# An encoder block on Trainium2: first and second gate products ahead of the third, merge loads behind branch A's last values, another tile order, operands realigned

## The chip, the cores and the metric

One core of one Trainium2 chip runs the whole program. The metric is the device time of one execution in microseconds (us). TensorE is called PE here, VectorE DVE, ScalarE ACT, GpSimd POOL, and SyncE, which issues most of the transfers (DMAs), SP.

## The reference

An encoder block on 1024 tokens of width 1024, with 16 meta tokens in front, in float32. Two attention branches read the same normalised input: A is a differential attention over all 1040 keys (4 heads, each with two softmaxes whose second is subtracted with a weight), B a grouped attention over a window with sinks. Each branch has a gate per element, a projection of the same input. After the merge come an output projection and a SwiGLU feed-forward network (FFN).

```python
h = jnp.concatenate([meta, x], axis=1)
# mixer_block(rms_norm(h)):
proj = h @ w_in                       # qa, ka, va, qb, kb, vb, ga, gb
y_a = differential_attention(qa, ka, va, ...)   # softmax(s1) - lam * softmax(s2), ALiBi bias
y_b = windowed_gqa(qb, kb, vb, sink)
merged = jax.nn.sigmoid(ga) * (y_a @ w_ba) + jax.nn.sigmoid(gb) * (y_b @ w_bb)
h = h + merged @ w_o
# swiglu(rms_norm(h)):
h = h + (jax.nn.silu(h @ w_gate) * (h @ w_up)) @ w_down
return rms_norm(h, norm_final)[:, N_META:]
```

## The kernel before, in words

**Arithmetic.** Every matrix operand is split into a high and a low float32 part (`split`, L116: ACT writes the high part, another engine the difference), and a product is three matmuls: high × high, high × low, low × high. The large products (gates, output projection, FFN) follow a Strassen–Winograd scheme: seven products of halves, numbered p = 1, 2, 6, 5, 7, 3, 4, in place of eight, with sums of halves before and after.

**Stages.** In the time of the trace: projections and branch B to about 294 us; branch A from there to 626 us, with the gate products filled in; the merge (`branch_w` L709, `branch_mm` L716, `gated` L1192) to 735 us; output projection and FFN norm to 816 us; FFN gate and up products (L1568) to 1243 us; down products (L1672) to the end.

**Branch A** runs over 32 tiles (head h, block t of 128 queries). `scores_a` (L922) makes for each of two softmaxes (m = 1, then 0) three chunks of scores, 352, 352 and 336 keys: the first two into the double bank `two` (one buffer), the third into a bank with the tag `sc` (three buffers). DVE adds the bias and takes the minimum (L942, L946), ACT takes the exponential (L950), and DVE combines the two (L956). `transpose_a` (L961) then turns the 1040 keys of that tile in blocks of four, four and one, again through `sc`, which ACT (L971) and DVE (L972) empty. `values_a` (L975) multiplies with the values for two tiles at a time, and `normed_a` (L985) norms four tiles. `load_a` (L900) loads queries and keys of a head (`aq`, `ak`) from DRAM.

**Gate products.** There are 8 pairs k of output columns with seven products each (`order_g`, L728–730). One product is four steps of three matmuls (`gate_steps`, L817, matmul at L850); its weights are loaded by `load_g` (L745), put together by `weights_g` (L759: p = 6 needs two sums on POOL, L779 and L780, p = 1 and 2 none) and split. p = 1 is kept in `u` tiles, p = 2 is stored, p = 6 is added to the kept p = 1 and stored to DRAM (`u_d`, L864), and is loaded again for the later products. The moving operand is the transposed input `hT_hi`, `hT_lo`, of whose four quarters (half of the contraction × half of the tokens) three are overwritten, one of them twice, by prepared sums `t_d`, here called T0, T1, T2 and T3: `turn_into` (L808). RIGHT_G (L802) says which quarter a product reads: p = 1 and 5 the quarter that T0 replaces, p = 2 and 4 that of T3, p = 3 the quarter that stays, and p = 6 and 7 the quarter of T2 and then T1. T0, T1 and T3 can come only when the first products of all pairs no longer need what lies there.

**Order.** The order of PE's instructions in branch A is written by hand: the string SLOTS (L41) gives the order in one tile, with s for a chunk of this tile's scores, t for a third of the tile before's transposition, n for a step of the tail (values, norm), g for one gate step. Ahead of a head stand G_FIRST = 24 (first head) or G_HEAD = 6 gate steps (L54), and HOLD = 22 steps are kept for the end. The order on the other engines, and that of the transfers on SP's queue, is set by a scheduler with a timeline of its own.

**Merge.** Its first loads are two blocks of `w_bb` (L711 into `m0`) and eight of `yb` (L1138 into `m1`); each `yb` block is split by ACT (L117) and DVE (L118) before the first matmul at L719. The loads of gates `gt` are issued at L1195, their sigmoid runs on ACT at L1196.

Of the kernel before, what the change touches and what calls it, by code (L numbers as in the profile page):

```python
# [37 lines left out]
N_WAIT = 3  # L38
PP2 = 2
COMBINE_POOL = (0, 1, 2, 3)  # L40
SLOTS = "ssgsgssgsngtntgnt"  # L41
SLOTS_LAST = "ssgsgssgsngtntgnt"
S_BUFS = (2, 2)
AT_BUFS = 2
G_BUFS = 3
HOLD = 22
GT_BUFS = 4
WB_BUFS = 6
# [25 lines left out]
def encoder_block(ctx: ExitStack, tc: tile.TileContext, x, meta, norm_mix, w_in, lq1, lk1, lq2, lk2,  # L74
# [7 lines left out]
    def f32(ap):  # L82
        return ap.bitcast(F32)
# [27 lines left out]
    ones = const.tile([P, 1], F32, name="ones")  # L111
    nc.gpsimd.memset(ones, 1.0)
    neg_half = const.tile([P, 4], F32, name="neg_half")
    nc.gpsimd.memset(neg_half, -0.5)

    def split(hi, lo, src, lo_eng):  # L116
# [591 lines left out]

    def branch_w(p, o, src, nme, raw=None, low=None):  # L709
        w = (raw_tile(f"wbr{nme}_{o}")[:, 0:512] if raw is None else raw).rearrange("p (c n) -> p c n", n=P)  # L710
        nc.sync.dma_start(w, src[:, o * P:(o + 1) * P].rearrange("(c p) n -> p c n", p=P))  # L711
        wh = p.tile([P, 2, 4, P], F32R, tag="wh", name=f"wbh{nme}_{o}", bufs=WB_BUFS)
        split(wh[:, 0], wh[:, 1], w, low or nc.gpsimd)
        return wh
# [11 lines left out]


    G_COLS = [C_GB + 2 * k * P for k in range(4)] + [C_GA + 2 * k * P for k in range(4)]  # L728
    first_g = [(k, p) for i in (0, 2) for p in (1, 2) for k in (i, i + 1)] + [(k, 6) for k in range(4)]
    first_g += [(k, p) for k in range(4, 8) for p in (1, 6, 2)]  # L730
    order_g = first_g + [(k, p) for k in range(8) for p in (5, 7, 3, 4)]
    n_first = len(first_g)

# [1 line left out]
    for n, (k, p) in enumerate(order_g):  # L735
        if n >= n_first:
            uses_g.append([("s", k, 1), ("s", k, 0)] if p == 5 else [])
        elif k < 4:
            uses_g.append({1: [("f", k, 0)], 2: [], 6: [("m", k, 0), ("m", k, 1)]}[p])
        else:  # L740
            uses_g.append({1: [("f", k, 0)], 2: [], 6: [("f", k, 1)]}[p])
    loads_g = [u for us in uses_g for u in us]
    raw_g, ops_g, n_loaded, n_freed, n_made = {}, {}, [0], [0], [0]

# [14 lines left out]
    def weights_g(n):  # L759
        k, p = order_g[n]  # L760
        load_g()
        tt = nc.gpsimd.tensor_tensor
        nm = f"{k}_{p}"
        kind = "s" if n >= n_first else "f" if k >= 4 or p != 6 else "m"
        wa, wb = raw_g[kind, k, 0], raw_g.get((kind, k, 1))
        a11, a12 = wa[:, 0:4], wa[:, 4:8]
        if wb is not None:
            a21, a22 = wb[:, 0:4], wb[:, 4:8]
        done = []
        if p == 1:  # L770
            src = a11
        elif p == 2:
            src, done = a12, ["f"]
            if k < 4:
                n_freed[0] += 1
            else:
                n_freed[0] += 2
        elif p == 6:
            tt(a21, a21, a22, ALU.add)  # L779
            tt(a21, a21, a11, ALU.subtract)  # L780
            src = a21
            if k < 4:
                n_freed[0] += 2
        elif p == 5:
            src = sums_g[k] = gstage.tile([P, 4, P], F32, tag="s", name=f"s1g_{k}", bufs=1)
            tt(src, a21, a22, ALU.add)
        elif p == 7:
            tt(a21, a11, a21, ALU.subtract)
            src = a21
        elif p == 3:  # L790
            tt(a12, a12, a11, ALU.add)
            tt(a12, a12, sums_g.pop(k), ALU.subtract)
            src = a12
        else:
            src = a22
# [7 lines left out]
            n_made[0] += 1  # L803

    RIGHT_G = {1: (0, 0), 6: (0, 1), 2: (1, 0), 5: (0, 0), 7: (0, 1), 3: (1, 1), 4: (1, 0)}
    INTO_T = {2: (0, 1), 0: (0, 0), 1: (0, 1), 3: (1, 0)}

    def turn_into(i):  # L808

        d, t = INTO_T[i]  # L810
        for hl, h in enumerate((hT_hi, hT_lo)):
            with ExitStack() as after:
                if i == 2:
                    after.enter_context(tc.issue_after(keys_a[0].ins))
                nc.sync.dma_start(f32(h)[:, 4 * d:4 * d + 4, HALF[t]], t_d[i][:, hl])

    def gate_steps():  # L817
        banks, kept = {}, {}
# [10 lines left out]
        add = nc.vector.tensor_tensor  # L829
        for n, (k, p) in enumerate(order_g):  # L830
            ensure_g(n + 1)
            if n == n_first - 4:
                kept[0] = kept_g("u_0")
                nc.sync.dma_start(kept[0], u_d[0])
            if n >= n_first - 1 and p in (2, 4) and (n < n_first or k < 7):
# [12 lines left out]
            for c in range(4):  # L848
# [3 lines left out]
                                     stop=(p in (2, 6, 3, 4) and c == 3 and i == 2), skip_group_check=True)  # L852
                if c == 3:
                    if p == 1:
                        kept[k] = kept_g(f"p1_{k}")
                        nc.scalar.copy(kept[k], ps)
                    elif p == 2:
                        st = stage_g(f"g11_{k}")
                        nc.scalar.copy(st, ps)
                        store(st, 2 * k, 0)  # L860
                    elif p == 6:
                        u = kept.pop(k)
                        add(u, ps, u, ALU.add)
                        nc.sync.dma_start(u_d[k], u)  # L864
                    elif p == 5:
                        kept["q"] = kept_g(f"q_{k}")
                        nc.scalar.copy(kept["q"], ps)
                    elif p == 7:
                        st = stage_g(f"g22_{k}")
                        add(st, ps, kept.pop("q"), ALU.add)  # L870
                        store(st, 2 * k + 1, 1)
                    else:
                        st = stage_g(f"g{p}_{k}")
                        if p == 3:
                            nc.scalar.copy(st, ps)
                        else:
                            add(st, ps, kept[k], ALU.add)
                        store(st, 2 * k + (p == 4), int(p == 3))
                    if n + 1 == n_first - 2:
                        turn_into(0)  # L880
                    elif n + 1 == n_first - 1:
                        turn_into(1)
                    elif n + 1 == n_first:
                        turn_into(3)
                    if p == 4:
                        del kept[k]
                    if p == 7 and k < 7:
                        kept[k + 1] = kept_g(f"u_{k + 1}")
                        nc.sync.dma_start(kept[k + 1], u_d[k + 1])
# [94 lines left out]

    def normed_a(h, c, py):  # L985
        nm = f"{h}_{c}"
        ysq = apool.tile([P, 512], F32, tag="ysq", name=f"ysq_{nm}", bufs=1)
        nc.scalar.activation(ysq, py, AF.Square)
        yg = apool.tile([P, 512], F32, tag="yg", name=f"yg_{nm}", bufs=2)
        nc.scalar.activation(yg, py, AF.Copy, scale=gsub)  # L990
        yield
        pst = bank(psum2, "sc", f"apst_{nm}", SC)
# [24 lines left out]
            next(gates, None)  # L1017


    acc = [None]  # L1020

    def turn(done):
        h, t, s, at_, v = done
# [2 lines left out]
    def later(done):  # L1026
        h, t, s, at_, v = done
        if t % 4 == 1:
            acc[0] = bank(psum2, "acc", f"apy_{h}_{t}", 1)
        yield from values_a(h, t, v, at_, acc[0])  # L1030
        if t % 4 == 3:
            yield from normed_a(h, t // 4, acc[0])

# [40 lines left out]
    while tail:  # L1074
        step_tail()
        fill(1)
    order_pe.__exit__(None, None, None)
    close_apool()
    fill(1000)
    bops, close_bops = pool("bops")  # L1080

    def half_op(p, name):
# [2 lines left out]
    def block_pair(i, name, dtype):  # L1085
        return bops.tile([P, 2, 4, 512], dtype, tag=f"x{i}", name=name, bufs=1)

    ypool, close_ypool = pool("ypool")
    close_psum2()
    close_stage()  # L1090
# [31 lines left out]
    m0, m1, ya0 = block_pair(0, "m0", F32), block_pair(1, "m1", F32), block_pair(2, "ya0", F32R)  # L1122
    a11, asum, a12, w11 = m0[:, 0], m0[:, 1], m1[:, 0], m1[:, 1]

    def merged(o, half):
        return ((a11, a21), (a12, a22))[o // 4][half][:, o % 4]

# [5 lines left out]

    yb_t = []
    for j in range(4):
        raws_b = a12[:, j], w11[:, j]
        for h in range(2):
            nc.sync.dma_start(raws_b[h], yb_d[j][:, h * 512:h * 512 + 512])  # L1138
# [666 lines left out]
```

## Time and profile before

| | us |
| --- | --- |
| three runs | 1461.11, 1463.01, 1465.54 |
| median | 1463.01 |
| profiled execution | 1460.98 |
| its span in the profile | 1458.9 |
| PE busy | 1419.6 (97%) |
| DVE, ACT, POOL busy | 913.6, 704.8, 603.2 |

Mean granted clock of PE: 0.987. The profile shows one execution. A line of a group names the line of the kernel, the engine, the operation, output <- inputs, the shape and the count, then busy time, mean ns of one, and the engine's idle time just before with what ended it. In a timeline the first two columns are start and length; a bracket gives the idle time before and its releaser. Matmuls overlap: the length of one (389 ns) is more than the distance to the next (about 230 ns). A name of a queue (SPq) marks the issue of a transfer, not its time in flight.

### The profile page before, as it was taken

To read this page: it belongs to the slowest core of one execution; us is meant where nothing else is said; L and a number is where in the kernel's file an instruction comes from. 1 tells how busy PE (TensorE), PEld (TensorE's weight loads), DVE (VectorE), ACT (ScalarE), POOL (GpSimd) and SP (SyncE) were. 2 spreads that over 40 slices of the span, in tenths; PEclk is the share of its full clock that TensorE was granted. 3 is DMA by queue.
4 is the path that set the end of the run, shared out by engine and by line. 5 is a ranking of instruction groups with operands and counts; after the bars stand their busy time and mean duration, and the time that the engine had idled before them with its cause. 6 is when DMAs were issued, how large, how long until landed. Compare 5 with 4: busy or idle time off the path is not lost.

```text
span 1458.9 us, 20686 instructions
## 1 busy us (share of the span) xinstructions
PE 1419.6 (97%) x7183; PEld 1209.3 (83%) x7183; DVE 913.6 (63%) x1584; ACT 704.8 (48%) x1340; POOL 603.2 (41%) x591
## 2 busy tenths in 40 slices
PE   9999999988999999979999999999999999999998
PEld 8998999976888888868888888888888888888886
DVE  6555666526676767735978866754455443787666
ACT  6355556434565555545345654333333333444444
POOL 4157866228364645230513135544544542000442
PEclk9999999998999999989999999999999999999999
DMA  8445564396558344186351633433333322964444
GB/s 235 97 123 154 165 194 136 101 292 202 168 191 261 128 148 150 44 295 205 131 178 58 195 107 110 144 123 97 100 100 104 99 94 102 327 221 135 132 124 144
DMA packets 190696, 222.98 MB, mean 153 GB/s; under 512 B 17064, under 2 KB 125040, under 8 KB 190592
## 3 DMA queue, kind: packets, MB, share of 16 engines
q1 hardware_dynamic: 188672, 218.84, 47.6%
q10 hardware_dynamic: 1920, 2.83, 0.7%
q8 instruction: 56, 0.92, 0.3%
q14 instruction: 48, 0.39, 0.1%
HBM read 150.64 MB, written 64.42 MB: 147 GB/s over the span
## 4 chain that ended last, share of the span: by engine, by line
PE 87%; DVE 5%; DMA 4%; ACT 2%; issue 1%; SPq 1%; POOL 0%; ACTq 0%; DVEq 0%; POOLq 0%
PE pg L1568 29%; PE pd L1672 14%; PE pg L850 6%; PE ppa L719 5%; PE po L1471 4%; PE aps L939 3%; PE pp_va L228 3%; PE pp_qb L228 3%; PE pp_qa L228 3%; PE apy L981 3%; PE pp_ka L228 3%; DMA ak<-ka_d 2%; PE bps L395 2%; PE po L1479 2%; PE bpy L435 1%; PE bpt L430 1%
## 5 line engine op out<-in xcount | busy, mean ns | idle before, releaser
L1568 PE MATMUL pg<-t,wop 128*128 128x512 f32 x1056 | 242.8, 389 | 0.0
L1568 PEld LDWEIGHTS pg<-t,wop 128*128 128x128 f32 x1056 | 198.2, 188 | 41.8
L118 POOL TENSOR_TENSOR wop<-wf,wop 128x512 fp32r<-128x512 f32 x114 | 152.7, 1341 | 168.1 <-ACT wop L117 156.2
L1672 PE MATMUL pd<-ob,oa 128*128 128x512 f32 x924 | 209.6, 389 | 0.0
L1672 PEld LDWEIGHTS pd<-ob,oa 128*128 128x128 f32 x924 | 173.4, 188 | 36.1 <-DVE ob L118 0.2
L1568 PE MATMUL pg<-b,wop 128*128 128x512 f32 x792 | 188.5, 395 | 0.0
L850 PE MATMUL pg<-hT_hi,wopg 128*128 128x512 f32 x448 | 174.7, 410 | 8.5 <-ACT wopg L117 7.8
L1568 PEld LDWEIGHTS pg<-b,wop 128*128 128x128 f32 x792 | 148.0, 187 | 36.1
L117 ACT ACTIVATE wop<-wf 128x512 fp32r<-128x512 f32 x128 | 80.8, 633 | 76.7 <-PE pg L1568 54.2
L950 ACT ACTIVATE as<-as,amn 128x1040 f32<-128x1040 f32 x64 | 74.4, 1163 | 64.9 <-DVE amn L946 64.7
L850 PEld LDWEIGHTS pg<-hT_hi,wopg 128*128 128x128 f32 x448 | 87.0, 194 | 22.4 <-ACT wopg L117 8.5
L118 POOL TENSOR_TENSOR oa<-ra,oa 128x512 fp32r<-128x512 f32 x27 | 34.9, 1294 | 168.9 <-ACT oa L117 167.4
L939 PE MATMUL aps<-ak,aq 128*128 128x352 f32 (+1 forms) x384 | 88.5, 338 | 13.1 <-DVE at L972 6.5
L117 ACT ACTIVATE oa<-ra 128x512 fp32r<-128x512 f32 x77 | 48.7, 632 | 107.9 <-PE pd L1672 45.6
L939 PEld LDWEIGHTS aps<-ak,aq 128*128 128x128 f32 x384 | 66.2, 192 | 30.7 <-DVE at L972 7.9
L942 DVE CUSTOM_DVE_ANT_0 as<-aps,dist,far_a 128x704 f32<-128x704 f32 x64 | 60.4, 944 | 48.2 <-PE aps L939 48.2
L850 PE MATMUL pg<-hT_lo,wopg 128*128 128x512 f32 x224 | 89.9, 402 | 0.0
L1345 DVE TENSOR_TENSOR s<-wf,wf 128x512 f32<-128x512 f32 x22 | 15.7, 714 | 114.8 <-DMA wf<-in_w_ff_up_dram 72.2
L397 DVE CUSTOM_DVE_ANT_0 bs<-bps,tbx,nsink 128x432 f32<-128x432 f32 (+1 forms) x64 | 38.5, 627 | 56.4 <-PE bps L395 35.0
L407 POOL TENSOR_SCALAR bs<-bs,bdn 128x432 f32<-128x432 f32 (+1 forms) x64 | 37.0, 597 | 76.7 <-DVE bdn L405 48.9
L1595 ACT COPY p<-pg 128x512 f32<-128x512 f32 x44 | 25.8, 585 | 66.5 <-PE pg L1568 62.3
L981 PE MATMUL apy<-at,av 128*128 128x256 f32 x400 | 57.4, 287 | 0.0
(320 smaller groups left out, 3148.5 us busy)
## 6 DMA issues: line engine op xcount, KB each, us to landing
ra<-aop SPq DMA_DIRECT2D x77, 256.0 KB, 2.7
wf<-in_w_ff_gate_dram SPq DMA_DIRECT2D x25, 512.0 KB, 3.9
wf<-in_w_ff_up_dram SPq DMA_DIRECT2D x25, 512.0 KB, 3.8
aop<-as SPq DMA_DIRECT2D x44, 256.0 KB, 2.2
w_c<-in_w_in_dram SPq DMA_DIRECT2D x17, 512.0 KB, 4.9
aop<-c SPq DMA_DIRECT2D x33, 256.0 KB, 2.0
t_d<-tst SPq DMA_DIRECT2D x16, 512.0 KB, 3.9
g_d<-g SPq DMA_DIRECT2D x32, 256.0 KB, 3.6
```

Source lines behind the costliest of these rows:

```text
L117: high = nc.scalar.activation(hi, src, AF.Copy)
L118: lo_eng.tensor_tensor(lo, src, f32(hi), ALU.subtract)
L228: product = nc.tensor.matmul(ps[:, :n], a[:, c, :], b[:, c, at:at + n], start=(u == 0), stop=(u == 3 * DC - 1))
L719: nc.tensor.matmul(ps, w[:, a, j, :], src(j, b, tk), start=(j == 0 and n == 0), stop=(j == 3 and n == 2))
L850: nc.tensor.matmul(ps, op[:, x, c, :], h[:, 4 * d + c, HALF[t]], start=(p in (1, 6, 7) and c == 0 and i == 0), stop=(p in (2, 6, 3, 4) and ...
L939: nc.tensor.matmul(ps[:, :n], qs[m][:, t * P:(t + 1) * P], ks[m][:, vv, k0:k0 + n], start=(vv == 0), stop=(vv == 1))
L942: nc.vector.tensor_tensor_reduce(s[m][:, 0:2 * n].rearrange("p (a k) -> p a k", a=2), two[:, :, :n], dist[:, u0:u0 + 2 * n].rearrange("p ( ...
L950: nc.scalar.activation(s[m][:, 0:L], s[m][:, 0:L], AF.Exp, bias=mn[:, m, 1:2], scale=-1.0, accum_out=dn[:, 1:2] if m else first_sum)
L981: nc.tensor.matmul(py[:, cols], v[:kp, a, k, :], at_[:kp, k, b, :], start=(k == 0 and j == 0), stop=(k == 8))
L1471: nc.tensor.matmul(sets_o[p][u], oa[:, a, u * P:(u + 1) * P], ob[:, b, :], start=(p in (1, 5) and j == 0 and k == 0), stop=(p in (2, 3) an ...
L1568: nc.tensor.matmul(ps, op[:, x, c, :], b[:, y, c, :], start=(p in (1, 5) and c == 0 and n == 0), stop=(p in (4, 2, 3) and c == 3 and n == ...
L1672: nc.tensor.matmul(ps[u], oa[:, a, u * P:(u + 1) * P], ob[:, b, :], start=(p in (1, 2, 5) and j == 0 and k == 0), stop=(p in (2, 3, 4) and ...
```

## The change

It has four parts.

1. A tile of 64 bytes for each partition, `room`, is allocated among the constants and never used. Tiles allocated after it on the left side of SBUF start 64 bytes further on.
2. The gate products p = 1 and p = 2 of all eight pairs come first, then p = 6 of all eight. Results of p = 1 go to DRAM and are loaded again one product ahead of its use. Every pair takes its p = 6 weights with two loads of its own (before: pairs 4 to 7 reused a load). T0 is loaded after product (7, 1), T3 in eight transfers during (7, 2), T1 after (7, 6); before, T0, T1 and T3 came with the last three of the first 24 products.
3. In a tile's order, the first n and the first t stand ahead of the second half of the scores.
4. The merge's first loads are issued as soon as the last values of branch A have been given out; branch A's pool is closed there, and two of its tiles (`ysq`, `yg`) move to another pool.

```diff
-SLOTS = "ssgsgssgsngtntgnt"
+SLOTS = "ssgsgntssgsgntgnt"
...
+ROOM = 16
...
+    const.tile([P, ROOM], F32, name="room")
...
-        nc.sync.dma_start(w, src[:, o * P:(o + 1) * P].rearrange("(c p) n -> p c n", p=P))
+        if raw is None:
+            nc.sync.dma_start(w, src[:, o * P:(o + 1) * P].rearrange("(c p) n -> p c n", p=P))
...
-    first_g = [(k, p) for i in (0, 2) for p in (1, 2) for k in (i, i + 1)] + [(k, 6) for k in range(4)]
-    first_g += [(k, p) for k in range(4, 8) for p in (1, 6, 2)]
+    first_g = [(k, p) for i in (0, 2, 4, 6) for p in (1, 2) for k in (i, i + 1)] + [(k, 6) for k in range(8)]
...
-        elif k < 4:
+        else:
             uses_g.append({1: [("f", k, 0)], 2: [], 6: [("m", k, 0), ("m", k, 1)]}[p])
-        else:
-            uses_g.append({1: [("f", k, 0)], 2: [], 6: [("f", k, 1)]}[p])
...
+    LAST_T = {(7, 1): 0, (7, 2): 3, (7, 6): 1}
...
-        for hl, h in enumerate((hT_hi, hT_lo)):
-            with ExitStack() as after:
-                if i == 2:
-                    after.enter_context(tc.issue_after(keys_a[0].ins))
-                nc.sync.dma_start(f32(h)[:, 4 * d:4 * d + 4, HALF[t]], t_d[i][:, hl])
+        for c in (range(4) if i == 3 else (slice(0, 4),)):
+            for hl, h in enumerate((hT_hi, hT_lo)):
+                with ExitStack() as after:
+                    if i == 2:
+                        after.enter_context(tc.issue_after(keys_a[0].ins))
+                    to = f32(h)[:, 4 * d:4 * d + 4, HALF[t]]
+                    nc.sync.dma_start(to[:, c], t_d[i][:, hl, c])
...
-            if n == n_first - 4:
-                kept[0] = kept_g("u_0")
-                nc.sync.dma_start(kept[0], u_d[0])
+            for k_next in [0] * (n in (n_first - 9, n_first - 2)) + [k + 1] * (p == 6 and k < 7):
+                kept[k_next] = kept_g(f"u_{k_next}")
+                nc.sync.dma_start(kept[k_next], u_d[k_next])
...
                     if p == 1:
-                        kept[k] = kept_g(f"p1_{k}")
-                        nc.scalar.copy(kept[k], ps)
+                        p1 = kept_g(f"p1_{k}")
+                        nc.scalar.copy(p1, ps)
+                        nc.sync.dma_start(u_d[k], p1)
...
-                    if n + 1 == n_first - 2:
-                        turn_into(0)
-                    elif n + 1 == n_first - 1:
-                        turn_into(1)
-                    elif n + 1 == n_first:
-                        turn_into(3)
+                    if (k, p) in LAST_T:
+                        turn_into(LAST_T[k, p])
...
-        ysq = apool.tile([P, 512], F32, tag="ysq", name=f"ysq_{nm}", bufs=1)
+        ysq = gstage.tile([P, 512], F32, tag="ysq", name=f"ysq_{nm}", bufs=1)
...
+        if (h, t) == (AH - 1, NT - 1):
+            valued.append(t)
...
     n_gates[0] += HOLD
+    while not valued:
+        step_tail()
+        fill(1)
+    close_apool()
+    bops, close_bops = pool("bops")
...
+    for o, raw in enumerate((a11[:, 2], asum[:, 0])):
+        nc.sync.dma_start(raw.rearrange("p (c n) -> p c n", n=P), w_bb[:, o * P:(o + 1) * P].rearrange("(c p) n -> p c n", p=P))
+    for j in range(4):
+        for h in range(2):
+            nc.sync.dma_start((a12, w11)[h][:, j], yb_d[j][:, h * 512:h * 512 + 512])
     while tail:
         step_tail()
         fill(1)
     order_pe.__exit__(None, None, None)
-    close_apool()
     fill(1000)
```

More of the change, by code (lines that the diff above doesn't have):

```diff
@@ L40 @@
 COMBINE_POOL = (0, 1, 2, 3)
-SLOTS = "ssgsgssgsngtntgnt"
-SLOTS_LAST = "ssgsgssgsngtntgnt"
+SLOTS = "ssgsgntssgsgntgnt"
+SLOTS_LAST = "ssgsgntssgsgntgnt"
 S_BUFS = (2, 2)
@@ L763, in weights_g @@
         nm = f"{k}_{p}"
-        kind = "s" if n >= n_first else "f" if k >= 4 or p != 6 else "m"
+        kind = "s" if n >= n_first else "m" if p == 6 else "f"
         wa, wb = raw_g[kind, k, 0], raw_g.get((kind, k, 1))
@@ L768, in weights_g @@
             a21, a22 = wb[:, 0:4], wb[:, 4:8]
-        done = []
         if p == 1:
@@ L772, in weights_g @@
         elif p == 2:
[L773 to L777, printed above, removed]
+            src = a12
+            n_freed[0] += 1
         elif p == 6:
@@ L781, in weights_g @@
             src = a21
-            if k < 4:
-                n_freed[0] += 2
+            n_freed[0] += 2
         elif p == 5:
@@ L831, in gate_steps @@
             ensure_g(n + 1)
-            if n == n_first - 4:
-                kept[0] = kept_g("u_0")
-                nc.sync.dma_start(kept[0], u_d[0])
-            if n >= n_first - 1 and p in (2, 4) and (n < n_first or k < 7):
+            for k_next in [0] * (n in (n_first - 9, n_first - 2)) + [k + 1] * (p == 6 and k < 7):
+                kept[k_next] = kept_g(f"u_{k_next}")
+                nc.sync.dma_start(kept[k_next], u_d[k_next])
+            if n == n_first - 1 or (p == 4 and k < 7):
                 nxt = 0 if n < n_first else k + 1
@@ L986, in normed_a @@
         nm = f"{h}_{c}"
-        ysq = apool.tile([P, 512], F32, tag="ysq", name=f"ysq_{nm}", bufs=1)
+        ysq = gstage.tile([P, 512], F32, tag="ysq", name=f"ysq_{nm}", bufs=1)
         nc.scalar.activation(ysq, py, AF.Square)
-        yg = apool.tile([P, 512], F32, tag="yg", name=f"yg_{nm}", bufs=2)
+        yg = gstage.tile([P, 512], F32, tag="yg", name=f"yg_{nm}", bufs=2)
         nc.scalar.activation(yg, py, AF.Copy, scale=gsub)
@@ L1017, in fill @@
             next(gates, None)
-    acc = [None]
+    acc, valued = [None], []
     def turn(done):
@@ L1073, in encoder_block @@
     n_gates[0] += HOLD
-    while tail:
+    while not valued:
         step_tail()
         fill(1)
-    order_pe.__exit__(None, None, None)
     close_apool()
-    fill(1000)
     bops, close_bops = pool("bops")
@@ L1086, in block_pair @@
         return bops.tile([P, 2, 4, 512], dtype, tag=f"x{i}", name=name, bufs=1)
+    m0, m1, ya0 = block_pair(0, "m0", F32), block_pair(1, "m1", F32), block_pair(2, "ya0", F32R)
+    a11, asum, a12, w11 = m0[:, 0], m0[:, 1], m1[:, 0], m1[:, 1]
+    for o, raw in enumerate((a11[:, 2], asum[:, 0])):
[3 more added lines that the diff above has]
+            nc.sync.dma_start((a12, w11)[h][:, j], yb_d[j][:, h * 512:h * 512 + 512])
+    while tail:
+        step_tail()
+        fill(1)
+    order_pe.__exit__(None, None, None)
+    fill(1000)
     ypool, close_ypool = pool("ypool")
@@ L1121, in encoder_block @@
     a21, a22 = (keep.tile([P, 4, 512], F32, name=f"m_{n}") for n in ("21", "22"))
-    m0, m1, ya0 = block_pair(0, "m0", F32), block_pair(1, "m1", F32), block_pair(2, "ya0", F32R)
-    a11, asum, a12, w11 = m0[:, 0], m0[:, 1], m1[:, 0], m1[:, 1]
     def merged(o, half):
@@ L1135, in encoder_block @@
     for j in range(4):
-        raws_b = a12[:, j], w11[:, j]
-        for h in range(2):
-            nc.sync.dma_start(raws_b[h], yb_d[j][:, h * 512:h * 512 + 512])
         yb_t.append(ybpool.tile([P, 2, S], F32R, name=f"yb{j}"))
```

## The prediction, given before the changed kernel was run

> **What bounds the kernel now.** I read the page first: busy time, clock, and the chain that ended last.
>
> ```profile
> PE 1419.6 (97%) x7183; PEld 1209.3 (83%) x7183; DVE 913.6 (63%) x1584; ACT 704.8 (48%) x1340; POOL 603.2 (41%) x591
> ...
> PEclk9999999998999999989999999999999999999999
> ...
> PE 87%; DVE 5%; DMA 4%; ACT 2%; issue 1%; SPq 1%; POOL 0%; ACTq 0%; DVEq 0%; POOLq 0%
> ```
>
> TensorE (PE) is busy for 97% of the span and holds 87% of the chain. The other engines matter only where PE waits for them. So there are three places to gain: idle time of PE, stretches at a lower clock (the two slices marked 8), and the pitch of the matmuls themselves. The waits of PE between 300 and 660 us, next, list all idle time that the change can reach (total, times, longest, in us).
>
> ```profile
> PE ppa L719 <- ACT yb L117: 7.9, 1, 7.9
> PE pg L850 <- ACT wopg L117: 7.8, 2, 6.0
> PE aps L939 <- DVE at L972: 6.5, 7, 2.1
> PE aps L939 <- DVE amn L942: 3.3, 7, 1.0
> PE aps L939 <- DMA ak<-ka_d: 3.2, 3, 1.7
> PE ppa L719 <- DVE yb L118: 0.6, 1, 0.6
> PE pg L850 <- POOL wopg L118: 0.5, 1, 0.5
> ```
>
> That is 29.8 us: 8.5 where the merge starts, 6.0 and 2.3 where a gate product waits for its weights, 9.8 at score matmuls that wait for a PSUM bank or buffer, 3.2 for keys still in flight. A longer stall costs clock as well. These are stretches from the windows view: length, busy time of PE, PEld, DVE, ACT, POOL, clock, DMA share, GB/s.
>
> ```profile
> 332.00:338.00 6.00, 5.88 (x19) 4.58 (x20) 1.66 (x3) 2.00 (x4) 4.71 (x4) 0.50 0.77 209
> ...
> 365.50:367.40 1.90, 1.90 (x7) 1.61 (x7) 1.01 (x4) 0.61 (x1) 0.69 (x1) 0.51 0.00 0
> ...
> 508.90:512.30 3.40, 3.40 (x13) 3.11 (x13) 1.85 (x7) 1.35 (x3) 0.07 (x1) 0.50 0.00 0
> 644.40:648.80 4.40, 3.80 (x8) 2.68 (x9) 4.40 (x7) 4.40 (x9) 0.76 (x1) 0.50 1.10 351
> ```
>
> PE works there at 0.50 of its clock, so half of each stretch is lost.
>
> **The change, part by part.** The sum is made against the profiled execution (1460.98 us, span 1458.9).
>
> *A, operands realigned.* The 64-byte tile `room` shifts what lies above it on the left side of SBUF. By the allocated addresses, the three moving operands `b` of FFN products (L1568) start at 64 modulo 128 before and at 0 after; their stationary operand `wop` starts at 0 in both. The same stationary tile with the moving operand `t`, at 0 already, is the comparison; `yb`, too, is out of step with its weights and `ya` is not.
>
> ```profile
> L1568 PE MATMUL pg<-t,wop 128*128 128x512 f32 x1056 | 242.8, 389 | 0.0
> L1568 PE MATMUL pg<-b,wop 128*128 128x512 f32 x792 | 188.5, 395 | 0.0
> ...
> L719 PE MATMUL ppa<-yb,wbhb 128*128 128x512 f32 x192 | 45.8, 401 | 8.5 <-ACT yb L117 7.9 <-DVE yb L118 0.6
> L719 PE MATMUL ppa<-ya,wbha 128*128 128x512 f32 x192 | 44.0, 390 | 0.2 <-DVE wbha L118 0.2
> ```
>
> `b` matmuls cost 6 ns more than `t` matmuls: 792 × 6 ns = **−4.75 us**. By busy time, 188.5/792 − 242.8/1056 = 8.1 ns, so −6.4 at most; nothing if alignment isn't the cause.
>
> *B, start of branch A.* The gate product that stood ready least was p=6 of pair 0: its two raw loads and two GpSimd sums came before its split.
>
> ```profile
> 323.97 0.80 PE L939 MATMUL aps<-ak,aq 128*128 128x352 f32 x4
> ...
> 331.78 0.80 PE L850 MATMUL pg<-hT_hi,wopg 128*128 128x512 f32 x1 [6.01 <-ACT wopg L117]
> ...
> 324.12 1.30 DVE L956 SCALAR_TENSOR_TENSOR as<-as,adn,as 128x1040 f32<-128x1040 f32 x1
> ```
>
> After the change p=1 or p=2 of a later pair stands there, which splits a loaded half without a sum. The 6.0 us go, and with them the half clock of 332 to 338 (6 us at 0.50: 3 us lost). Late next is the first transposition, which now stands ahead of tile 1's second scores (at 323.97) and needs tile 0's combination (324.12 + 1.30 = 325.42): 1.5 us, with a hand-over some 1.7, and about 1.4 for a short clock stretch. Net **−5.9** (−9 to 0).
>
> *C, the tiles.* With `t` earlier, score banks are evicted earlier (L972), so most of the 9.8 us at L939 goes, and two clock stretches of 3.4 us like that at 509.
>
> ```profile
> 365.30 0.69 PE L939 MATMUL aps<-ak,aq 128*128 128x336 f32 x2 [2.12 <-DVE at L972]
> ...
> 386.46 0.47 PE L939 MATMUL aps<-ak,aq 128*128 128x336 f32 x2
> 386.77 0.39 PE L850 MATMUL pg<-hT_hi,wopg 128*128 128x512 f32 x1
> ...
> 387.47 0.60 PE L968 MATMUL apt<-ident,as 128*128 128x128 f32 x4
> ...
> 389.47 1.24 PE L981 MATMUL apy<-at,av 128*128 128x256 f32 x9
> ...
> 389.46 1.30 DVE L956 SCALAR_TENSOR_TENSOR as<-as,adn,as 128x1040 f32<-128x1040 f32 x1
> ```
>
> The new exposure is the softmax. The last scores of tile 7 start at 386.46 and its combination ends at 389.46 + 1.30 = 390.76: 4.3 us. In the new order PE has between these four gate steps (386.77 to 387.47: 0.70 each, 2.8), the next tile's three score parts (1.1 by the rows of tile 7 in D), the rest of a transposition (0.5) and one or two parts of values (1.1 each): 5.5 to 6.6 us. That covers it; I keep 5.7 us for new waits, 0.7 in each of the eight tiles in which the row sums' own transposition (L1005) still holds a score bank. 9.8 + 2 × 1.7 − 5.7 = 7.5: **−7.5** (−12 to +15, the latter in the rivals).
>
> The rows disagree here with the Trainium skill, "TensorE: Matmul & The Clock Gate", Part 1 on the HAM clock gate: it has the clock fall after an idle window of about 3.4 us. Here a wait of 2.12 us was followed by 0.51. By the page the two stretches would have another cause, and this term would be some 3 us smaller.
>
> *D, the boundary of heads 0 and 1.* This speaks against the change. Keys and queries of head 1 are loaded during tile 7. So far little is queued before them on SP; the last keys are 1.04 us late.
>
> ```profile
> 383.99 0.34 SPq L906 DMA_DIRECT2D aq<-qa_d  x1
> ...
> 387.82 1.11 SPq L909 DMA_DIRECT2D ak<-ka_d  x2
> ```
>
> ```profile
> 382.01 0.89 PE L939 MATMUL aps<-ak,aq 128*128 128x352 f32 x4
> ...
> 397.10 0.32 PE L939 MATMUL aps<-ak,aq 128*128 128x352 f32 x1
> 398.46 0.75 PE L939 MATMUL aps<-ak,aq 128*128 128x352 f32 x3 [1.04 <-DMA ak<-ka_d]
> ```
>
> The quarters T0 and T3 of hT (2.1 MB each) used to be reloaded well after that, in a stretch of their own:
>
> ```profile
> 425.56 0.38 SPq L815 DMA_DIRECT2D hT_lo<-t_d  x1
> 426.04 0.46 SPq L815 DMA_DIRECT2D hT_hi<-t_d  x1
> ```
>
> And the DMA view of 424 to 446:
>
> ```profile
> DMA packets 4050, 6.49 MB, mean 295 GB/s; under 512 B 124, under 2 KB 1148, under 8 KB 4047
> ...
> hT_hi<-t_d SPq DMA_DIRECT2D x3, 1024.0 KB, 8.2
> ```
>
> Now all 16 first and second products come first, so T0 is free after (7,1) and T3 after (7,2), in tiles 6 and 7. In SP's new order T0, five transfers of 256 KB, two weight loads of 512 KB and the eight chunks of T3 stand ahead of or between head 1's loads: with these (3.1 MB), 10.2 MB from T0 to the last keys. The window above moved 6.49 MB in 22 us, 2 of them idle: 325 GB/s. 10.2 MB take 31 us; T0 is issued some 5 us before tile 7's start, so the last keys land 26 us after it and are needed at 397.1 − 382.0 = 15.1: 11 us of stall. At 400 GB/s it would be 5.5. I take 10, nearer the measured rate, less today's 1.0, plus 2.5 for the clock (half of a 5 us stretch): **+11.5** (0 to +16).
>
> *E, T1* is loaded after (7,6) now, one product ahead of (0,7), which uses it. Cover: four of a tile's five gate steps, and 32 tiles take 302 us (324 to 626): 4/5 × 9.4 = 7.5. Load: 8.2 us to landing (the last row above) and 1.6 for a 512 KB weight load in front: 9.8. **+3** with its clock (0 to +5).
>
> *F, merge's loads* move from 627.43 to the end of the last values, some 6 us earlier. But ACT's order keeps four sigmoids and a weight split ahead of the first `yb`:
>
> ```profile
> 627.43 0.99 SPq L711 DMA_DIRECT2D m<-in_w_branch_b_dram  x2
> ...
> 640.38 2.72 ACT L1196 ACTIVATE gt<-gt 128x512 f32<-128x512 f32 x4 [4.72 <-DMA gt<-g_d]
> 643.17 0.63 ACT L117 ACTIVATE wbhb<-wbrb 128x512 fp32r<-128x512 f32 x1
> 643.71 4.25 ACT L117 ACTIVATE yb<-m 128x512 fp32r<-128x512 f32 x8
> ```
>
> Their `gt` loads are not moved ahead by as much; I expect the first `yb` at about 641: **−3** (−8 to 0).
>
> *At nothing:* eight more stores and eight loads of 256 KB and four of 512 KB, 6 MB in all, elsewhere hidden under the gate steps (if that cover goes, as in D); matmul, GpSimd and ACT counts are equal.
>
> Sum: −4.75 − 5.9 − 7.5 + 11.5 + 3 − 3 = −6.65. The profiled execution would take 1454.3 us; it stands 2.0 below the median of 1463.01, so I predict **1456**.
>
> **The rivals.**
>
> *R1, head 1's loads arrive in time,* because the transfers move faster than in the window above or T0 goes out sooner. For it: some half-microsecond slices of that window reach 400 GB/s and over. Against it: 10.2 MB in 20 us would need 510. D falls to +1 at most, and E may shrink: 1456 − 12 = 1444.
>
> *R2, slower: the softmax becomes the bound of each tile.* Where the first `t` comes before the combination of the tile before is done, PE waits in every tile; it decides from the point where the latency is above the cover of 5.5 to 6.6 us. With half a us in each of 30 tiles, +15: 1471. For it: DVE and ACT also get the evictions of `t` in the same stretch, in front of the exponential. Against it: 4.3 us in the rows above.
>
> *R3, the realignment does nothing:* `b` matmuls stay at 395 because of something else in those products. Then 1456 + 4.75 = 1461. Against it: `t` and `b` share weights, shape and line. The Trainium skill speaks for this rival: "TensorE: Matmul & The Clock Gate", Step-by-step, gives PE two independent read ports, one for the moving operand and one for weights, so that where the two lie relative to each other should not matter. The rows at 389 and 395 agree with this only if something other than the address separates them.
>
> **How the numbers follow.** Chances: the forecast 0.50 (its own range 1450 to 1462), R1 0.25, R2 0.13, R3 0.12. A measurement of this kernel tells a difference of 0.3% (4.4 us) from none. Faster by more than that, under 1458.6, are R1, and about three quarters of the forecast: 0.62. Slower, over 1467.4, is most of R2: 0.12. The rest, 0.26, is R3 and the forecast's upper end. The range takes in R1 and its better side of F, and the nearer part of R2: 1440 to 1470.
>
> **What the profile after would show.** A: `pg<-b` at 389. B: no wait of 6 us near 325, instead `apt` waiting for DVE at L956. C: L939 without DVE waits; if `apt` waits in most tiles, R2. D: a wait of `aps` for DMA of 8 to 12 us at tile 8, with a clock of 0.5 behind it; under 3 us means R1. E: a wait for `hT` near 510. F: the merge's wait for `yb` at 4 to 5 us. The forecast fails most easily in D: it hangs on one rate.

## The result, and the profile after

| | before | after |
| --- | --- | --- |
| runs, us | 1461.11 to 1467.81 (5) | 1450.25 to 1455.74 (5) |
| median, us | 1464.21 | 1452.44 |
| profiled execution, us (span) | 1460.98 (1458.9) | 1455.20 (1453.4) |

The ratio is 0.9922, with a 95% interval from 0.9898 to 0.9947: faster by 7.8 to 14.9 us, where 6.65 in a profiled execution and 1456 as the median were forecast. The executions of one kernel differ by 5 to 7 us here, and by 14 in the longest series (27 runs of before, 1458.1 to 1472.0). The profiled execution of before was faster than all five of its runs in the table, and that of after slower than three of the other four, so the 5.8 us between these two probably understate the gain. Sums of terms go by this profiled pair, and kernels are compared by their ratios to before, which was run again on the chip of each.

The page of after: busy time, clock by slice, and the chain.

```profile
PE 1413.3 (97%) x7183; PEld 1210.1 (83%) x7183; DVE 914.0 (63%) x1584; ACT 702.2 (48%) x1340; POOL 604.3 (42%) x591
...
PEclk9999999999999999999999999999999999999999
...
PE 83%; DMA 6%; DVE 4%; SPq 2%; issue 2%; ACT 1%; POOL 1%; ACTq 0%; DVEq 0%; POOLq 0%
```

PE is busy 6.3 us less for the same 7183 matmuls. DMA and SP's queue have 8% of the chain in place of 5%: transfers now end waits that others ended before. PE's waits between 300 and 660 us show which.

```profile
PE aps L934 <- DMA ak<-ka_d: 6.3, 2, 4.8
PE ppa L722 <- ACT yb L119: 6.2, 1, 6.2
PE apt L963 <- DVE at L967: 4.7, 5, 2.0
PE apt L963 <- DVE as L951: 3.2, 4, 1.3
PE aps L934 <- issue: 2.7, 1, 2.7
PE pg L848 <- ACT wopg L119: 2.4, 1, 2.4
PE aps L934 <- DVE at L967: 1.4, 1, 1.4
PE aps L934 <- DVE amn L937: 1.3, 4, 0.4
PE pg L848 <- POOL wopg L120: 0.5, 1, 0.5
```

Together 28.7 us, against 29.8 before. The wait of 6.0 us for weights is gone (the 2.4 is the old gap at 309 us), keys take 6.3 in place of 3.2, and DVE ends as much waiting as before, 10.6 against 9.8, though most of it at the transposition now (`apt`); the longest piece is 2.0 us (2.1 before). So little of the gain lies in PE's total idle time. The FFN groups show where the largest part that can be read off one row lies:

```profile
L1569 PE MATMUL pg<-t,wop 128*128 128x512 f32 x1056 | 242.4, 389 | 0.0
...
L1569 PE MATMUL pg<-b,wop 128*128 128x512 f32 x792 | 183.3, 389 | 0.0
```

The rest was read from the start of the same matmuls in both traces. From the start of tile 1 to that of tile 2: 15.12 us before, 8.55 after (−6.6). Tile 7 to tile 9: 22.23 against 35.83 (+13.6). From tile 2 to the last scores without that stretch: −7.1. Last scores to the first output projection: 125.2 against 123.9 (−1.2). FFN gate and up products: 426.4 against 420.8 (−5.6). Tile 0 starts 1.6 us later (316.3 and 317.9; 314.9 in one kernel below that has the same projections). These give −5.3; PE's last instruction is 5.4 us earlier.

One border moves with the change: the new order puts four transposition matmuls, and a wait of 1.6 us (0.7 before), ahead of the last scores. Measured to and from the start of the last tile instead, behind which both kernels have the same 561 matmuls, the −7.1 becomes −8.4 and the −1.2 becomes 0.0.

### The profile page after: what moved, and what is told of

The parts are those of the page before. It is cut to its first block, busy times and chain, and to the rows that moved or that the text cites. A ratio compares the mean times of both kernels' runs of the same rounds, so it can differ in the third digit from the quotient of the medians.

```text
span 1453.4 us, 20758 instructions
## 1 busy us (share of the span) xinstructions
PE 1413.3 (97%) x7183; PEld 1210.1 (83%) x7183; DVE 914.0 (63%) x1584; ACT 702.2 (48%) x1340; POOL 604.3 (42%) x591
## 4 chain that ended last, share of the span: by engine, by line
PE 83%; DMA 6%; DVE 4%; SPq 2%; issue 2%; ACT 1%; POOL 1%; ACTq 0%; DVEq 0%; POOLq 0%
PE pg L1569 29%; PE pd L1673 14%; PE pg L848 6%; PE ppa L722 5%; PE po L1472 4%; PE pp_va L230 3%; PE pp_qa L230 3%; PE aps L934 3%; PE pp_ka L230 3%; PE apy L976 3%; PE bps L397 2%; PE apt L963 2%; PE pp_qb L230 2%; PE po L1480 2%; PE bpy L437 1%
## 5 line engine op out<-in xcount | busy, mean ns | idle before, releaser
L1569 PE MATMUL pg<-b,wop 128*128 128x512 f32 x792 | 183.3, 389 | 0.0
L120 POOL TENSOR_TENSOR oa<-ra,oa 128x512 fp32r<-128x512 f32 x27 | 34.9, 1294 | 168.6 <-ACT oa L119 167.2
L966 ACT ACTIVATE at<-apt 128x512 fp32r<-128x512 f32 (+1 forms) x96 | 45.5, 484 | 42.1 <-PE apt L963 41.7
L976 PEld LDWEIGHTS apy<-at,av 128*128 128x128 f32 x400 | 56.0, 196 | 4.3
```

The lines of the kernel that those rows point to most:

```text
L120: lo_eng.tensor_tensor(lo, src, f32(hi), ALU.subtract)
L976: nc.tensor.matmul(py[:, cols], v[:kp, a, k, :], at_[:kp, k, b, :], start=(k == 0 and j == 0), stop=(k == 8))
L1569: nc.tensor.matmul(ps, op[:, x, c, :], b[:, y, c, :], start=(p in (1, 5) and c == 0 and n == 0), stop=(p in (4, 2, 3) and c == 3 and n == ...
```

## The experiments

### The 64 bytes alone, and four other offsets

`room_alone` is the kernel before with this alone:

```diff
+ROOM = 16
+    const.tile([P, ROOM], F32, name="room")
```

> The kernel before with the unused 64-byte tile alone. Theory (a moving operand out of step with the stationary one by 64 bytes modulo 128 costs 6 ns a matmul): the b products go from 395 to 389 ns, and the time falls by 4.5 to 6 us; nothing else moves by over 1 us. Rival (something else in the b products): 395 ns stay, and the time is within 1.5 us of before.

Measured: ratio 0.9957 (0.9935 to 0.998), −6.3 us, with the `b` products at 389 ns. Four kernels are the changed one with ROOM = 32, 8, 48 and 64 (128, 32, 192 and 256 bytes). The last three ran once each (1461.5 to 1462.1 us) and serve for the row below alone.

> The changed kernel with an unused tile of 128 bytes in place of 64, so that the FFN's moving operands b lie at 64 modulo 128 again. Theory (the offset modulo 128 against the stationary operand counts): b products at 395 ns again, 4.5 to 6 us slower than the changed kernel. Rival (any shift does, or the place in a larger bank): 389 ns stay, within 1.5 us of the changed kernel.

> The changed kernel with the unused tile at 32 bytes: b lies at 96 modulo 128, and at 96 modulo 256 with wop at 128. If only an offset of 64 modulo 128 costs, b products take 389 ns; if every offset below 128 costs, 391 to 395.

> The changed kernel with the unused tile at 192 bytes: b lies at 0 modulo 128 and at 0 modulo 256, while wop lies at 128 modulo 256. If the period is 128 bytes, b products take 389 ns as with 64; if it is 256 (128 bytes of room gave 392, not 395, so a longer period is open), 391 to 395.

> The changed kernel with the unused tile at 256 bytes: b lies at 64 modulo 256, as in the kernel before. If the period is 256 bytes, b products take 395 ns as before; if only something else made the 395, such as what else shares the left side at those places, 389 to 392.

The same row of the groups, one fence each for `room_alone` and 128, 32, 192 and 256 bytes:

```profile
L1570 PE MATMUL pg<-b,wop 128*128 128x512 f32 x792 | 183.3, 389 | 0.0
```

```profile
L1569 PE MATMUL pg<-b,wop 128*128 128x512 f32 x792 | 185.3, 392 | 0.0
```

```profile
L1569 PE MATMUL pg<-b,wop 128*128 128x512 f32 x792 | 188.5, 396 | 0.0
```

```profile
L1569 PE MATMUL pg<-b,wop 128*128 128x512 f32 x792 | 188.1, 395 | 0.0
```

```profile
L1569 PE MATMUL pg<-b,wop 128*128 128x512 f32 x792 | 188.4, 394 | 0.0
```

`wop` starts at 128 modulo 256. `b` starts there only with 64 bytes of room, and only then the products take 389 ns. At 96, 0, 64 and 64 (32, 192, 256 bytes and before) they take 394 to 396, at 192 (128 bytes) 392. So the period is not the 128 bytes that I argued from: with 192 bytes both lie at 0 modulo 128, and it does not help. All rows fit a period of 256. The gate products speak against 512: by the addresses, half of their moving operands lie 256 bytes off their weights modulo 512 and half lie even, and both halves start one matmul every 230 ns (median).

`wop` does not move in these kernels, so the rows alone can't tell whether `b`'s own place counts or its place relative to `wop`. The merge can. Before the change, `yb` and `ya` started at 64 modulo 256, as `b` did, but so did their weights, and at whole clock 24 of either's matmuls took 5.44 us, 227 ns each; `b` took 233 and `t` 227. So the relative place counts. (The prediction has `yb` out of step with its weights. By the addresses it was not; its 401 ns came from the stretch at half clock at the start of the merge, and in `yb_first` below, without that stretch, they are 392.) Which of the two reads waits for the other is not shown.

`room_128` took 392 ns, which neither side of its expectation has. It came out at 0.9934 (0.9912 to 0.9957), within its interval of the changed kernel; only its matmul row separates them.

### The tile order, in the changed kernel and alone

`old_slots` is the changed kernel, `new_slots_alone` the kernel before, each with the other's order. This is the edit of `old_slots`; that of `new_slots_alone` is its reverse:

```diff
-SLOTS = "ssgsgntssgsgntgnt"
+SLOTS = "ssgsgssgsngtntgnt"
```

> The changed kernel with the old order in a tile. Theory (the new order takes away the waits for score banks): the score matmuls wait 8 to 10 us for DVE again, two stretches at half clock come back, the transposition's waits of 7.9 us go; net 3 to 8 us slower than the changed kernel. Rival (the stall at head 1 ends when the keys land, and swallows what the tiles before it lose or gain; after it the two orders are equal): within 2 us of the changed kernel.

> The kernel before with the new order in a tile alone. The old order inside the changed kernel cost 19 us, where I had put the tile order at 7.5. Theory 1 (the order itself is worth more than the waits that it removes): 12 to 20 us under before. Theory 2 (7 to 10 us of it are the removed waits for score banks, and the rest came from the old order under the new gate order, where a late key wait shifts tiles against the gate steps): 5 to 10 us under before.

Measured: `old_slots` 1.0054 (1.0033 to 1.0074), slower than before, and some 19 us slower than the changed kernel. Neither side of its expectation held. `new_slots_alone` 0.9959 (0.994 to 0.9979), −6.0 us: its second theory. Waits of PE in `old_slots`:

```profile
PE aps L934 <- DMA ak<-ka_d: 11.3, 8, 2.8
PE aps L934 <- DVE at L967: 10.3, 7, 3.9
PE pg L848 <- ACT wopg L119: 6.0, 2, 3.5
PE aps L934 <- DMA g_d<-g: 4.9, 1, 4.9
```

and in `new_slots_alone`:

```profile
PE pg L850 <- ACT wopg L117: 6.6, 2, 4.7
PE apt L968 <- DVE at L972: 4.6, 4, 1.7
PE apt L968 <- DVE adn L953: 3.7, 1, 3.7
PE pg L850 <- POOL wopg L118: 3.3, 2, 2.7
```

By itself the new order removes the waits of score matmuls for banks. In the traces three tiles (5, 16 and 20) get 2.3 to 3.5 us shorter by it, but tiles 1 to 3 get 6.2 longer, by later weights and by a wait of 3.7 us for the softmax (`adn`); the profiled execution is only 2.1 us below that of before. The new gate order without it loses 15.3 us from tile 7 to 9 and then more: 5.7 us at tile 12 and 3.8 at head 2 (starts of tiles against before). So the parts are not a sum: under a backlog of transfers the old order loses what the new one rides out. Why, beyond the rows, stays argued.

### Who is late at head 1

`late_t` is the changed kernel with T0 and T3 behind head 1's keys:

```diff
-    LAST_T = {(7, 1): 0, (7, 2): 3, (7, 6): 1}
+    LAST_T = {(1, 6): 0, (2, 6): 3, (7, 6): 1}
...
-                    if i == 2:
-                        after.enter_context(tc.issue_after(keys_a[0].ins))
+                    if i != 1:
+                        after.enter_context(tc.issue_after(keys_a[i != 2].ins))
```

> The changed kernel with the reloads of T0 and T3 given out after products (1, 6) and (2, 6), and ordered behind head 1's keys on SP's queue; nothing else differs. Theory (the stall at head 1 comes from T0 and T3 standing ahead of its keys): the waits of the score matmuls for keys at tiles 8 and 9 (4.8 + 1.5 us, with the 2.7 and 1.4 us waits around them) fall to 2 us or less, the slow clock between 389 and 410 us goes, and the time falls by 10 to 14 us, to about 1440. Rival 1 (it is the volume of the reordered loads: u and the second weight halves fill the queue, whatever stands first): the wait for keys stays over 5 us, and the time moves by less than 4 us. Rival 2 (the reloads only collide with something later): keys come in time, but a gate product near 420 us waits 5 us or more for its weights or for T0, and the gain is under 6 us.

Measured: 0.9865 (0.9837 to 0.9893), 8 us below the changed kernel by the two ratios, a little under the theory's 10. Its waits, and the clock behind them:

```profile
PE aps L934 <- DMA ak<-ka_d: 4.3, 2, 2.3
...
PE aps L934 <- issue: 1.0, 1, 1.0
```

```profile
389.00:399.00 10.00, 8.02 (x31) 6.96 (x30) 3.81 (x9) 2.37 (x4) 3.76 (x3) 0.67 1.04 326
```

5.3 us are left of the changed kernel's 9.0, where the theory had 2 or less, and the slow clock did not go: 10.2 us at half clock lie there as in the changed kernel. No gate product waits for its weights later. So rival 2 falls, and rival 1 holds for a part: something besides T0 and T3 delays the keys. On the changed kernel `late_t` gains 5.0 us from tile 7 to 9 and 2.7 at tile 12.

`no_gates` undoes the whole new gate order in the changed kernel, with the loads and reloads that belong to it:

```diff
-    first_g = [(k, p) for i in (0, 2, 4, 6) for p in (1, 2) for k in (i, i + 1)] + [(k, 6) for k in range(8)]
+    first_g = [(k, p) for i in (0, 2) for p in (1, 2) for k in (i, i + 1)] + [(k, 6) for k in range(4)]
+    first_g += [(k, p) for k in range(4, 8) for p in (1, 6, 2)]
...
```

> The changed kernel without the new order of the gate products (old product order, old reloads; the tile order, the 64 bytes and the merge's loads as changed). Theory (the gate order gives some 5 us at the start of branch A and costs some 13 at head 1): PE waits 5 to 7 us again for the weights of pair 0's third product near 330 us, keys of head 1 are at most 3 us late, and the time is 5 to 10 us below the changed kernel. Rival (the orders need each other: the tile order gains only where the gate weights come early): 0 to 5 us above the changed kernel.

Measured: 0.9891 (0.986 to 0.9923), 4.5 us below the changed kernel by the ratios, whose intervals overlap: near the theory's 5, and not above the changed kernel as its rival has it. The waits are those of the theory: 6.7 us for weights near 330 (4.2 and 2.5) under the half clock, none to speak of for keys.

```profile
PE pg L853 <- ACT wopg L119: 6.6, 2, 4.2
...
PE pg L853 <- POOL wopg L120: 3.1, 2, 2.5
...
PE aps L942 <- DMA ak<-ka_d: 0.4, 1, 0.4
```

So the gate order, as it was put in, costs about as much as it brings, or more.

### ACT's order at the merge, and the best version

In `yb_first` the first sigmoids, the split of later `w_bb` blocks and those of `ya` are ordered behind the splits of `yb` on ACT:

```diff
-                    split(yb_t[k][:, 0, cols], yb_t[k][:, 1, cols], (a12, w11)[h][:, k], nc.vector)
+                    yb_high.append(split(yb_t[k][:, 0, cols], yb_t[k][:, 1, cols], (a12, w11)[h][:, k], nc.vector))
...
-        gate_ops.append(nc.scalar.activation(gt, gt, AF.Sigmoid))
+        with tc.issue_after(yb_high[-1].ins):
+            gate_ops.append(nc.scalar.activation(gt, gt, AF.Sigmoid))
```

> The changed kernel with ACT's order at the merge mended: the eight splits of yb ahead of the first four sigmoids, the split of the third w_bb block and those of ya. Theory (the loads moved ahead gained little because the splits of yb stand behind ACT's wait for a later w_bb block and for ya, which land at 641.9 and 643.3 us, while the last yb landed at 634.9): PE's wait at the first merge product falls from 6.2 us to 1 or 2, and the time falls by 4 to 6 us. Rival (the splits wait for the room that the last gate products hold, or for DVE): the wait stays above 4.5 us, gain under 1.5 us.

The changed kernel's ACT before the merge, in its timeline:

```profile
641.90 0.63 ACT L119 ACTIVATE wbhb<-wbrb 128x512 fp32r<-128x512 f32 x1 [2.25 <-DMA wbrb<-in_w_branch_b_dram]
643.29 0.63 ACT L119 ACTIVATE ya<-raw_ya 128x512 fp32r<-128x512 f32 x1 [0.76 <-DMA raw_ya<-ya_d]
643.83 4.25 ACT L119 ACTIVATE yb<-m 128x512 fp32r<-128x512 f32 x8
```

and that of `yb_first`, with PE's waits there:

```profile
634.65 2.19 ACT L119 ACTIVATE yb<-m 128x512 fp32r<-128x512 f32 x4
```

```profile
PE ppa L722 <- DVE yb L120: 2.2, 3, 1.2
...
PE ppa L722 <- ACT yb L119: 0.8, 1, 0.8
```

The wait falls from 6.2 to 3.0 us in four small pieces (1 or 2 were expected), and no slow clock follows. From the last scores to the output projection it takes 118.8 us, 5.2 less than the changed kernel, as the theory has it. By runs it is 0.991 (0.9878 to 0.9942), which cannot show 5 us against 0.9922.

`late_all` is `late_t` and `yb_first` together, with pair 4's `m` weights behind head 1's keys too (the line that it adds to those two):

```diff
-                    after.enter_context(tc.issue_after(keys_a[0].ins))
+                    after.enter_context(tc.issue_after(keys_a[n_loaded[0] > 16 and len(keys_a) > 1].ins))
```

> The changed kernel with three things together: T0 and T3 behind head 1's keys as in late_t, the weights of pair 4's third product behind them too, and ACT's order at the merge as in yb_first. Theory (the terms add): late_t's gain of 8 to 10 us, some 2 us more at tile 8, and 4 to 6 us at the merge: 14 to 18 us under the changed kernel, PE's idle time between 290 and 740 us about 15 us in place of 29. Rival (keys are bound by their own transfer time after the queries' tile comes free): no gain at tile 8 over late_t, 12 to 14 us in all.

Measured: 0.9841 (0.9811 to 0.9871), median 1439.68: below both kernels, by some 12 us below the changed one. PE idles 20.1 us between 290 and 740 us (29.5 in the changed kernel), where 15 were expected; keys cost 2.8. The 12 us miss the theory's 14 to 18 and are the rival's number, but the rival's reason does not hold: from tile 7 to 9 it takes 25.9 us, 30.9 in `late_t`, so the keys were not bound by their own transfer. From tile 9 to 10, 1.4 us of this are lost again.

```profile
PE aps L934 <- DMA ak<-ka_d: 2.8, 3, 1.6
PE ppa L722 <- DVE yb L120: 2.1, 3, 1.2
...
PE ppa L722 <- ACT yb L119: 0.8, 1, 0.8
```

`no_gates_yb` is its rival, `no_gates` with `yb_first`'s edit.

> The changed kernel without the new order of gate products, but with ACT's order at the merge mended as in yb_first. It is late_all's rival for the best version. Theory (the new gate order, once its reloads stand behind head 1's keys, keeps only its gain at the start of branch A): the wait near 330 us stays (6 to 7 us with slow clock), the merge's goes, 1441 to 1444 us, 2 to 5 us above late_all. Rival (the gate order is worth nothing even when mended): equal to late_all within 1 us.

Measured: 0.9872 (0.9847 to 0.9896). That is 4.5 us above `late_all` in ratio, as the theory has it, but the intervals overlap: that the mended gate order is worth something is likely and not settled.

## Why the prediction was right, point by point

**A, −4.75: right in size, with the wrong period.** −6.3 us by runs, −5.6 in the stage, −5.2 by busy time. The rule "64 modulo 128" gave the right result here by luck: 128 is not the period, and `yb`, its second example, was misread. The Trainium skill ("TensorE: Matmul & The Clock Gate", Step-by-step) gives PE two independent read ports, by which the place of one operand relative to the other would do nothing. The five offsets, with `yb` and `ya` beside them, speak against that for these operands.

**B, −5.9: −6.6 at its place,** and the late next was the one named: the first transposition waits 1.32 us for L951. But it is not the gate order's alone. From tile 1 to tile 2 it takes 15.1 us before, 13.1 with the new gate order and the old tile order (`old_slots`, where a wait of 3.5 us for weights stays), 16.9 the other way round (`no_gates`), and 8.6 with both. The step "which splits a loaded half without a sum" left out that this half lands late as well.

**C, −7.5: −7.1 in the pair (−8.4 to the start of the last tile), −6.0 alone.** Right in size, but +2.6 us at tile 12 are in it that belong to the backlog under D; without them it is −9.7 (−11.0). The reason held in these tiles and not beside them. Of the 9.8 us of waits for DVE 8.7 lay here before, and 5.0 do after, 2.0 of them at tile 12. The rest of the 10.6 after stands in tile 1 (1.3), at head 1 (2.1) and in and behind the last tile (2.3). At the score matmuls 2.7 are left; the others moved to the transposition. The slow stretches at 366 and 509 us went, and one at 435 came. In this window of after the clock is whole:

```profile
508.00:515.00 7.00, 7.00 (x47) 6.52 (x46) 6.18 (x13) 2.91 (x8) 5.37 (x6) 1.00 0.19 75
```

The 3.4 us idle window of the Trainium skill ("TensorE: Matmul & The Clock Gate", Part 1) is not a safe bound here: 2.00 us of idle time that ended at 434.1 were followed by a stretch at half clock (435.0 to 438.4). The Trainium skill says there that the window runs free; it would fit that 3.28 us of idle time in `no_gates_yb` (at 352) were followed by none.

**D, +11.5: +13.6, at the place and by the way foretold.** SP's queue and PE at the boundary in after:

```profile
368.09 0.37 SPq L813 DMA_DIRECT2D hT_lo<-t_d  x1
...
393.25 1.57 SPq L904 DMA_DIRECT2D ak<-ka_d  x2
```

```profile
389.05 0.40 PE L934 MATMUL aps<-ak,aq 128*128 128x352 f32 x1 [2.72 <-issue]
394.24 1.25 PE L934 MATMUL aps<-ak,aq 128*128 128x352 f32 x3 [4.79 <-DMA ak<-ka_d]
...
401.02 0.40 PE L934 MATMUL aps<-ak,aq 128*128 128x352 f32 x1 [1.38 <-DVE at L967]
402.96 0.72 PE L934 MATMUL aps<-ak,aq 128*128 128x352 f32 x3 [1.54 <-DMA ak<-ka_d]
```

T0 goes out at 368.1, 4.8 us before tile 7; the last keys are there when PE's last wait for them ends, at 402.96, 34.9 us later (31 forecast). PE waits 10.4 us in all (10 forecast): 6.3 for keys by name, 2.7 with no releaser named, which end as the first keys have landed (388.96), and 1.4 for an eviction. That 10 and 10.4 agree is in part luck. The last keys came 30.1 us after tile 7's start and not 26, and PE needed them later than forecast, since two stretches at half clock, 10.2 us, lie on its way (they cost 5.1; 2.5 was too little):

```profile
389.00:399.00 10.00, 5.16 (x21) 4.53 (x22) 2.23 (x5) 0.87 (x1) 0.00 (x0) 0.66 1.05 333
399.00:410.00 11.00, 8.08 (x40) 6.98 (x39) 5.11 (x11) 3.64 (x8) 4.15 (x5) 0.84 0.98 276
```

The one rate on which it hung held: 327 GB/s from 366 to 402 us, where I took 325.

```profile
DMA packets 8845, 11.76 MB, mean 327 GB/s; under 512 B 487, under 2 KB 5033, under 8 KB 8843
```

What was short were the bytes: 11.5 MB moved between T0's issue and that last wait, where I took 10.2 (and the transfers that I listed come to 9.7).

Five more traces have the same gate and tile order and the same queue (`yb_first` and the four other sizes of `room`). They take 36.7 to 39.8 us from tile 7 to 9, where after takes 35.8, so differences of single traces here are good to some 4 us.

`late_t` shows that T0's and T3's place in the queue did 5.0 or more of the 13.6, and `late_all`, with pair 4's weights behind the keys too, takes off 4.9 more (1.4 of them come back at the next tile). The last 3.7 are not separated: other reordered loads, or keys asked for sooner by faster tiles. What I left out: the backlog goes on to tile 12. POOL, ACT and PE there, in order of the chain:

```profile
430.83 1.28 POOL L781 TENSOR_TENSOR s1g<-wg_s 128x512 f32<-128x512 f32 x1 [3.95 <-DMA wg_s<-in_w_in_dram]
...
432.14 0.63 ACT L119 ACTIVATE wopg<-s1g 128x512 fp32r<-128x512 f32 x1 [5.05 <-POOL s1g L781]
...
434.13 0.63 PE L963 MATMUL apt<-ident,as 128*128 128x128 f32 x4 [2.00 <-DVE at L967]
```

Weights that no matmul needs yet are late, and ACT stands 5.05 us at their split. ACT's eviction of a transposed block is behind it (432.68), DVE's of the same block waits 2.29 us for that, and PE for DVE: +2.6 us from tile 11 to 12, and none in `late_t`. So D in all is +16.2, against 11.5.

**E, +3: 0.** No wait for `hT` in after. T1 was given out near 448 us and not 510; its load took 8.1 us, and the cover held. In `yb_first` it took 10.6 and PE waited 1.4; in the four kernels with other sizes of `room` PE waited 1.1 to 1.6. So the term was over-sized, and the 0 is in part luck.

**F, −3: −1.2, or 0.0 from the start of the last tile.** The step that failed is "I expect the first `yb` at about 641". It began at 643.83, no earlier than before (643.71), with its data there since about 635. The price was set by ACT's order, which I had read, but for the wrong neighbours: a later `w_bb` block and `ya`, both waiting for transfers, also stood ahead. In `new_slots_alone` this stretch takes 132.9 us (130.1 before and after), so the early loads may have paid for what the tile order costs there; one trace does not settle it.

The sum thus came out near its own measure (−6.65 against −5.8 between the profiled executions) and that is in part luck: D was 2 us too small in tiles 7 to 9 and nearly 5 with tile 12, F promised 2 to 3 too much, and E's 3 and C's surplus made up for them. The rivals: R1 falls by the rows of D, R3 by `room_alone`; R2 by the 3.2 us that `apt` waited for L951 in four tiles of 32. What remains open is where the rest of the 11.4 us lies that the ratio gives: the pair, a fast execution of before and a slower one of after, shows 5.8 of them, and no trace shows the others. The forecast of 1456 stands 3.6 us above the measured median.

## What to carry to other kernels

When transfers are issued in one queue, add up the bytes from the first moved one to the one that is needed next and divide by the rate of a busy stretch: that gave the cost at head 1 within a fifth in the profiled pair and within two fifths in the five traces like it, with the bytes counted short. A reload that has become possible early should still be ordered behind what is needed soon, and so should an in-order engine's work on data that is still in flight. Parts of a change can lean on one another, so undo each within the whole as well as trying it alone.

## What the runs showed of the hardware

A 128x512 matmul took 389 ns (in the pair before and after) when its moving operand and its stationary operand started at the same place modulo 256 bytes, and 392 to 396 ns at the four other offsets tried, 5 us over 792 matmuls. In the merge's products both at 64 were as good as both at 128 (227 ns from one start to the next). In the clock records of the 14 kernels here the slow stretches last 3.4, 6.8 or 10.2 us, but for the last of each, which runs past the kernel's end; whether an idle time is followed by one is not settled by its length alone: 2.00 us in the changed kernel was, 3.28 us in `no_gates_yb` was not.
